# Middle layer normalisation: the fourth deferred projection in a bank of its own, and the small statistics steps on VectorE with only the power left on GpSimd

## The chip, the cores and the metric

One Trainium2 chip, of which the kernel uses one core. The metric is the device time of one launch in microseconds (us), taken as the median of several runs. An execution taken by the profiler has a time of its own; the sums of the prediction are made on that execution.

## The reference, cut to what matters

Two transformer blocks run one after the other on 256 tokens of width 1024, in float32. The first has a mixer, a SwiGLU, another mixer, another SwiGLU and a closing norm; the change does not touch it. The second block is this loop over two layers:

```python
def layer_norm(x, g, b):
    mu = jnp.mean(xf, axis=-1, keepdims=True)
    var = jnp.mean(jnp.square(xf - mu), axis=-1, keepdims=True)
    y = (xf - mu) * lax.rsqrt(var + LN_EPS) * g + b
...
for l in range(DEPTH):
    mix = diff_attention(...) if l == 0 else chunk_attention(...)
    x = layer_norm(DEEPNORM_ALPHA * x + mix, ln_g[l, 0], ln_b[l, 0])
    x = layer_norm(DEEPNORM_ALPHA * x + swiglu_2(x, ffn_w_in[l], ffn_w_out[l]), ln_g[l, 1], ln_b[l, 1])
```

So there are four layer norms. Below they are called norm 0 (behind the first attention), norm 1 (behind the first SwiGLU of this block, the middle one), norm 2 (behind the second attention) and the last norm (behind the last SwiGLU, at the end of the kernel).

## The kernel before, in words

Activations lie with features on the partitions: eight blocks of 128 features by 256 tokens, kept in pairs. Every matmul of a projection is made in three parts to keep float32 precision: the weight is split into `hi` and `lo`, the activation likewise, and `mm3` (lines 245 to 250) issues hi by hi, hi by low activation, and lo by hi. A projection of one 128-feature output block is therefore 8 x 3 = 24 matmuls. `weights` (line 235) loads one weight tile, ScalarE writes `hi` (line 240), VectorE writes `lo` (line 243); `hi` and `lo` have six buffers each, so this work runs some tiles ahead of TensorE.

Accumulators lie in the eight banks of PSUM: three with the tag `pa`, and five for the rest: `s0`, `s1`, `po` (one each) and `tr` (two).

The norms 0 to 2 are objects of the class `Norm` (line 505). While the output blocks of the mixer or SwiGLU in front come out, VectorE forms z, ScalarE forms z times the norm's gain, the two are split, and sums of z and of its square are gathered. Two sets of 128x1 matmuls (line 352) add them over the features. Then come the small steps on a 128x2 tile, one column for each half of the tokens: VectorE copies the sums out of PSUM (`st`, line 527), GpSimd squares the mean, subtracts, floors and adds the epsilon (line 365), raises to the power -1/2 (line 368) and multiplies the mean by the result (`mr`, line 533). TensorE spreads both columns over all partitions with four transposes (`spread`, line 613, into `po`), and ScalarE copies them to `rm` (line 537).

The projections behind a norm do not wait for `rm`. `project` (line 553) runs its 24 matmuls on z times gain, which is not normalised yet, and corrects the result afterwards: VectorE copies two correction columns (`dc`, line 561), multiplies by the reciprocal deviation out of `rm` (line 563, the last reader of the bank), and adds the mean's part (line 564). So a projection's bank stays taken until `rm` is there. `self.tags` is a list of banks for the first projections of a norm, taken one by one in line 554; when it is empty, a projection takes a `pa` bank. Norms 0 and 2 get the list `FOUR`, whose fourth entry is `tr`. Norm 1 gets no list:

```python
    FOUR = ("pa", "pa", "pa", "tr")
    ln = Norm(src, gen, 0, "po", FOUR)
    ln = Norm(ln, ffn(ln, I["v1_0"], I["v3_0"], I["v2_0"], None), 1, 'po')
```

Behind norm 1 stands `chunk_mixer`. Its steps are written out in order: "h0 h1 n0 v0 c0 h2 c1 v1 h3 c2 c3". The step h0 runs four projections (two of keys, two of queries; here p1 to p4), then the scores of four heads; h1 runs four more (p5 to p8); n0 writes the normalised activations themselves (line 548 and 549, on VectorE, held back behind the last query tile of h0); v0 is a projection of the values with them (lines 302 to 304), which takes two `pa` banks at once.

`last_norm` (line 568) ends the kernel; its rows are not deferred. It shares `rpow` (line 362) with the class `Norm`, and these two are all that call it with `floor` set.

The order of the instructions on each engine is made at build time by a list scheduler that plays the program through with its own estimates of durations. Each engine then runs its own list in that order. The program names the engine of each step, the banks, and a few orders such as the one that holds n0 back; the scheduler places the rest.

Of the kernel before, what the change touches and what calls it, by code (L numbers as in the profile page):

```python
# [12 lines left out]
ALU = mybir.AluOpType  # L13
# [150 lines left out]
def model(tc, I, out):  # L164
    with ExitStack() as es:
        _model(es, tc, I, out)


def _model(es, tc, I, out):
    nc = tc.nc  # L170
    V, A, T, G = nc.vector, nc.scalar, nc.tensor, nc.gpsimd
# [10 lines left out]
    class State:  # L182
        def __init__(self):
            self.t = [None] * 4
# [50 lines left out]
    def weights(ap, n):  # L235
        raw = wr.tile([128, n], F32, tag="w", name="raw")
        nc.sync.dma_start(out=raw, in_=ap)
        hi = wh.tile([128, n], F32R, tag="w", name="hi")
        with hold_act():
            A.activation(hi, raw, AF.Copy)  # L240
        lo = wl.tile([128, n], F32R, tag="w", name="lo")
        with hold_dve():
            V.tensor_tensor(out=lo, in0=raw, in1=hi.bitcast(F32), op=ALU.subtract)  # L243
        return hi, lo

    def mm3(ps, hi, lo, k, h, first, last):
        a, b = hi[:, k * 128:k * 128 + 128], lo[:, k * 128:k * 128 + 128]
        T.matmul(ps, a, h[0], start=first, stop=False, skip_group_check=True)  # L248
        T.matmul(ps, a, h[1], start=False, stop=False, skip_group_check=True)  # L249
        T.matmul(ps, b, h[0], start=False, stop=last, skip_group_check=True)  # L250
# [4 lines left out]
    def bank():  # L255
        return pa.tile([128, 2, S], F32, tag="pa", name="pa")

    def att(tag, shape=(128, 512)):
        if tag == "sc":
            turn[0] ^= 1  # L260
            tag = f"s{turn[0]}"
        return pt.tile(list(shape), F32, tag=tag, name=tag, bufs=PB[tag])

    def big(name="b", dt=F32):
        return bp.tile([128, 2, S], dt, tag="big", name=name)
# [41 lines left out]
    def hpair():  # L307
        return [hp.tile([128, 2, S + 2], F32R, tag=t, name=t) for t in ("hh", "hl")]
# [48 lines left out]
    def square(src, n):  # L357
        sq = sp.tile([128, 2, S], F32, tag="sq", name="sq", bufs=4)[:, 0:n]
        A.activation(sq, src, AF.Square)
        return sq  # L360

    def rpow(v, n, eps, floor=False):
        r = sp.tile([128, n], F32, tag="rp", name="rp", bufs=6)
        if floor:
            G.tensor_scalar(out=r, in0=v, scalar1=0.0, scalar2=eps, op0=ALU.max, op1=ALU.add)
        else:
            G.tensor_scalar(out=r, in0=v, scalar1=eps, scalar2=None, op0=ALU.add)
        G.tensor_tensor(out=r, in0=r, in1=mhalf[:, :n], op=ALU.pow)
        return r
# [32 lines left out]
    def two(ap, n=2):  # L402
        return ap.unsqueeze(1).to_broadcast([128, n, S])
# [3 lines left out]
    def ffn(H, w1, w3, w2, rb):  # L407
        gs, acc = [], []

        def down(f0, f1, last):  # L410
            for o, (d0, n) in enumerate(OUT):
                if len(acc) <= o:
                    acc.append(att(("sc", "sc", "tr", "tr", "po")[o], (128, n, S)))
                for j in range(n):
                    hi, lo = weights(w2[d0 + j][:, f0 * 128:f1 * 128], (f1 - f0) * 128)
                    for k in range(f0, f1):
                        mm3(acc[o][:, j], hi, lo, k - f0, gs[k], k + j == 0, last and k == f1 - 1)
                if last:
                    yield d0, n, acc[o]

        def gate(p1, p3, n, bias=None, up=None):
            s = wk.tile([128, 2, S], F32, tag="ev", name="fs", bufs=4)[:, 0:n]
            if bias is not None:
                A.activation(s, p1, AF.Silu, bias=bias)
            elif rb is None:
                A.activation(s, p1, AF.Silu)
            else:
                a = wk.tile([128, 2, S], F32, tag="ev", name="fa", bufs=4)
                V.tensor_tensor(out=a, in0=p1, in1=two(rb), op=ALU.mult)
                A.activation(s, a, AF.Silu)  # L430
                V.tensor_tensor(out=s, in0=s, in1=two(rb), op=ALU.mult)
            gg = wk.tile([128, 2, S], F32, tag="ev", name="fg", bufs=4)[:, 0:n]
            if up is None:
                V.tensor_tensor(out=gg, in0=p3, in1=s, op=ALU.mult)
            else:
                V.scalar_tensor_tensor(out=gg, in0=p3, scalar=up, in1=s, op0=ALU.add, op1=ALU.mult)
            return gg

        def up(f0, f1, H):
            for f in range(f0, f1, 2):  # L440
                p1, p3 = bank(), bank()
                for j in range(2):
                    for ps, w in ((p1, w1), (p3, w3)):
                        hi, lo = weights(w[f + j], 1024)
                        for k in range(8):
                            mm3(ps[:, j], hi, lo, k, H[k], k == 0, k == 7)
                gg = gate(p1, p3, 2)
                g = [big("gh", F32R), big("gl", F32R)]
                split(gg, g)
                gs.extend((g[0][:, j], g[1][:, j]) for j in range(2))  # L450

        def deferred(f0, f1):
            for f in range(f0, f1):
                a, ab = H.project(w1, f)
                b, bb = H.project(w3, f)
                gg = gate(a.unsqueeze(1), b.unsqueeze(1), 1, ab, bb)
                if f % 2 == 0:
                    g = [big("gh", F32R), big("gl", F32R)]
                o = [x[:, f % 2] for x in g]
                split(gg[:, 0], o)  # L460
                gs.append(o)

        for f0, f1 in ((0, 8), (8, 16), (16, NFF)):
            if rb is None:
                deferred(f0, f1)
            else:
                up(f0, f1, H)
            yield from down(f0, f1, f1 == NFF)
            if f0 == 0 and rb is None:
                H.normalize(False)  # L470
# [31 lines left out]
    class Norm:  # L502
        def __init__(self, src, gen, idx, tag, tags=()):
            self.gcol, self.bcol = V_LNG + idx * 8, V_LNB + idx * 8
            self.zg, self.HD = State(), []
            self.tags = list(tags)
            stats = Stats((ncol, mcol), tag)
            for d, n, ps in gen:
                z = wk.tile([128, 2, S], F32, tag="t2", name="z", bufs=3)[:, 0:n]
                V.scalar_tensor_tensor(out=z, in0=src.Y.at(d, n), scalar=ALPHA, in1=ps, op0=ALU.mult, op1=ALU.add)  # L510
                zg = self.zg.at(d, n)
                for j in range(n):
                    A.activation(zg[:, j], z[:, j], AF.Copy, scale=vec[:, self.gcol + d + j:self.gcol + d + j + 1])
                if d % 2 == 0:
                    hl = hpair()
                    for i in range(2):
                        G.tensor_copy(hl[i][:, :, S:S + 2], gbs[i].bitcast(F32)[:, idx, d:d + 2])
                o = [x[:, d % 2:d % 2 + n, 0:S] for x in hl]
                split(zg, o)
                self.HD += [(hl[0][:, (d + j) % 2], hl[1][:, (d + j) % 2]) for j in range(n)]  # L520
                stats.add(0, z, d, n)
                stats.add(1, square(z, n), d, n)
            stats.total(0)
            stats.total(1)
            hold_act.set(recent[1], 3, 3)
            st = sp.tile([128, 4], F32, tag="st4", name="st4")
            V.tensor_copy(st, stats.ps)
            v = sp.tile([128, 2], F32, tag="v2", name="v2", bufs=6)
            G.tensor_tensor(out=v, in0=st[:, 0:2], in1=st[:, 0:2], op=ALU.mult)
            G.tensor_tensor(out=v, in0=st[:, 2:4], in1=v, op=ALU.subtract)  # L530
            r = rpow(v, 2, 1e-5, True)
            mr = sp.tile([128, 2], F32, tag="mr", name="mr")
            G.tensor_tensor(out=mr, in0=st[:, 0:2], in1=r, op=ALU.mult)
            pb = att("po", (128, 2, S))
            spread([r, mr], pb)
            self.rm = wk.tile([128, 2, S], F32, tag="t2", name="rm", bufs=3)
            A.activation(self.rm, pb, AF.Copy)
# [650 lines left out]
    FOUR = ("pa", "pa", "pa", "tr")  # L1188
# [4 lines left out]
    src = Source()  # L1193
    src.Y, gen = diff_mixer(X)
    ln = Norm(src, gen, 0, "po", FOUR)
    ln = Norm(ln, ffn(ln, I["v1_0"], I["v3_0"], I["v2_0"], None), 1, 'po')

    def chunk_mixer(ln):
        v, M, hl = [], [], []
# [85 lines left out]
    ln = Norm(ln, chunk_mixer(ln), 2, "po", FOUR)  # L1285
# [17 lines left out]
```

## Time and profile before

| | us |
|---|---|
| median of 3 runs | 1304.98 (1304.94 to 1304.99) |
| the profiled execution, its own time | 1302.92 |
| its span, first to last instruction | 1301.1 |
| TensorE busy in the span | 1284.6 |
| VectorE busy | 941.3 |
| ScalarE busy | 708.5 |
| GpSimd busy | 45.7 |

Names in the profile: PE is TensorE's matmuls and PEld its weight loads, DVE is VectorE, ACT is ScalarE, POOL is GpSimd, SP is the queue that issues the loads. The profiled execution's own time is 1.82 us above its span, and 2.06 us below the median of the runs. A row of a timeline reads: start in us, duration in us, engine, line, operation, what is written and from what, its shape; xN joins N instructions that follow one another; in square brackets stands how long the engine was idle before it and what ended that. Matmuls overlap one another, so their starts tell more than their durations.

### The profile page before, as it was taken

How to read it: one execution, taken by the hardware profiler on the slowest of the kernel's cores; microseconds unless marked ns; L12 is line 12 of the kernel's file. 1: busy time of each engine (PE TensorE's matmuls, PEld its weight loads, DVE VectorE, ACT ScalarE, POOL GpSimd, SP SyncE). 2: the span in 40 equal slices, each digit the busy share in tenths (PEclk: the TensorE clock that was granted, in tenths of full speed). 3: DMA queues.
4: the chain of work that ended last, by engine and by line, in shares of the span. 5: the costliest groups of instructions: out<-in, count | busy, mean ns of one | idle time of the engine just before them, and what ended most of it. 6: DMA issues, size and time to landing. Idle time of an engine off the chain costs nothing.

```text
span 1301.1 us, 27363 instructions
## 1 busy us (share of the span) xinstructions
PE 1284.6 (99%) x11068; PEld 1240.3 (95%) x11068; DVE 941.3 (72%) x1759; ACT 708.5 (54%) x1185; POOL 45.7 (4%) x99
## 2 busy tenths in 40 slices
PE   9999999999999999999999999999999999999997
PEld 8979999999989999999999899999998889999997
DVE  7896775645888667465678869777779757968676
ACT  6684644434644455343468866544456656554443
POOL 1000000000000000000000021000000000000001
PEclk9999999999999999999999999999999999999999
DMA  9523665655643446565555345565554543655550
GB/s 315 190 82 111 204 201 182 186 183 150 213 155 122 126 167 206 183 186 188 162 178 183 118 130 178 155 209 162 189 174 167 171 138 122 219 187 185 181 158 37
DMA packets 65502, 219.69 MB, mean 169 GB/s; under 512 B 7520, under 2 KB 7904, under 8 KB 65376
## 3 DMA queue, kind: packets, MB, share of 16 engines
q1 hardware_dynamic: 65088, 217.82, 52.4%
q8 instruction: 87, 1.43, 0.4%
q14 instruction: 39, 0.32, 0.1%
q10 hardware_dynamic: 288, 0.12, 0.0%
HBM read 216.86 MB, written 1.05 MB: 167 GB/s over the span
## 4 chain that ended last, share of the span: by engine, by line
PE 97%; ACT 1%; DVE 1%; DMA 0%; issue 0%; SPq 0%; POOL 0%; ACTq 0%; DVEq 0%
PE pa L248 13%; PE pa L249 13%; PE pa L250 13%; PE pd L248 7%; PE pd L250 7%; PE pd L249 7%; PE s L248 4%; PE s L250 4%; PE s L249 4%; PE tr L248 3%; PE tr L249 3%; PE tr L250 3%; PE pv L302 2%; PE pv L303 2%; PE pv L304 2%; PE tr L613 1%
## 5 line engine op out<-in xcount | busy, mean ns | idle before, releaser
L240 ACT ACTIVATE hi<-raw 128x1024 fp32r<-128x1024 f32 (+3 forms) x420 | 424.1, 1018 | 484.8 <-PE pa L249 165.5
L243 DVE TENSOR_TENSOR lo<-raw,hi 128x1024 fp32r<-128x1024 f32 (+3 forms) x420 | 489.9, 1173 | 242.5 <-ACT hi L240 236.4
L248 PE MATMUL pa<-hh,hi 128*128 128x256 f32 x1424 | 401.7, 284 | 0.8 <-DVE ksw L800 0.5
L249 PE MATMUL pa<-hl,hi 128*128 128x256 f32 x1424 | 402.3, 283 | 0.0
L250 PE MATMUL pa<-hh,lo 128*128 128x256 f32 x1424 | 401.2, 283 | 0.0
L249 PEld LDWEIGHTS pa<-hl,hi 128*128 128x128 f32 x1424 | 268.6, 189 | 2.5 <-issue 0.6
L248 PEld LDWEIGHTS pa<-hh,hi 128*128 128x128 f32 x1424 | 267.2, 188 | 3.3 <-issue 1.1
L250 PEld LDWEIGHTS pa<-hh,lo 128*128 128x128 f32 x1424 | 268.6, 189 | 1.4 <-issue 0.7
L250 PE MATMUL pd<-hh,lo 128*128 128x258 f32 x752 | 212.9, 284 | 0.0
L248 PE MATMUL pd<-hh,hi 128*128 128x258 f32 x752 | 211.2, 284 | 1.6 <-DVE y L563 1.6
L249 PE MATMUL pd<-hl,hi 128*128 128x258 f32 x752 | 212.2, 283 | 0.0
L248 PEld LDWEIGHTS pd<-hh,hi 128*128 128x128 f32 x752 | 141.4, 189 | 2.0 <-DVE y L563 1.9
L249 PEld LDWEIGHTS pd<-hl,hi 128*128 128x128 f32 x752 | 142.8, 190 | 0.0
L250 PEld LDWEIGHTS pd<-hh,lo 128*128 128x128 f32 x752 | 142.2, 189 | 0.2
L250 PE MATMUL s<-gh,lo 128*128 128x256 f32 x352 | 97.4, 279 | 0.0
L249 PE MATMUL s<-gl,hi 128*128 128x256 f32 x352 | 97.4, 279 | 0.0
L248 PE MATMUL s<-gh,hi 128*128 128x256 f32 x352 | 95.8, 279 | 0.0
L249 PE MATMUL tr<-gl,hi 128*128 128x256 f32 x264 | 73.8, 280 | 0.0
L248 PE MATMUL tr<-gh,hi 128*128 128x256 f32 x264 | 73.8, 279 | 0.0
L250 PE MATMUL tr<-gh,lo 128*128 128x256 f32 x264 | 73.7, 279 | 0.0
L250 PEld LDWEIGHTS s<-gh,lo 128*128 128x128 f32 x352 | 65.9, 188 | 0.0
L249 PEld LDWEIGHTS s<-gl,hi 128*128 128x128 f32 x352 | 65.9, 187 | 0.0
(360 smaller groups left out, 1903.5 us busy)
## 6 DMA issues: line engine op xcount, KB each, us to landing
raw<-w SPq DMA_DIRECT2D x120, 512.0 KB, 3.8
raw<-v SPq DMA_DIRECT2D x120, 512.0 KB, 4.0
raw<-w_e SPq DMA_DIRECT2D x18, 512.0 KB, 4.8
raw<-w_aqk SPq DMA_DIRECT2D x16, 512.0 KB, 3.6
raw<-w SPq DMA_DIRECT2D x16, 384.0 KB, 3.2
raw<-v SPq DMA_DIRECT2D x16, 384.0 KB, 3.2
raw<-w_of SPq DMA_DIRECT2D x8, 512.0 KB, 4.2
raw<-w_oq SPq DMA_DIRECT2D x8, 512.0 KB, 3.6
```

The source lines that it names most:

```text
L240: A.activation(hi, raw, AF.Copy)
L243: V.tensor_tensor(out=lo, in0=raw, in1=hi.bitcast(F32), op=ALU.subtract)
L248: T.matmul(ps, a, h[0], start=first, stop=False, skip_group_check=True)
L249: T.matmul(ps, a, h[1], start=False, stop=False, skip_group_check=True)
L250: T.matmul(ps, b, h[0], start=False, stop=last, skip_group_check=True)
L302: T.matmul(ps[t], xh, a, start=k == 0, stop=False)
L303: T.matmul(ps[t], xh, b, start=False, stop=False)
L304: T.matmul(ps[t], xl, a, start=False, stop=k == 7)
L613: T.transpose(ps, src, ident)
```

## The change

In `rpow`, the step that floors the variance and adds the epsilon moves from GpSimd to VectorE where `floor` is set. In `Norm`, the square of the mean, the subtraction and the product `mr` move from GpSimd to VectorE; the power stays on GpSimd. Norm 1 gets the list `FOUR`, so its fourth projection takes a `tr` bank in place of a `pa` bank.

```diff
     def rpow(v, n, eps, floor=False):
         r = sp.tile([128, n], F32, tag="rp", name="rp", bufs=6)
         if floor:
-            G.tensor_scalar(out=r, in0=v, scalar1=0.0, scalar2=eps, op0=ALU.max, op1=ALU.add)
+            V.tensor_scalar(out=r, in0=v, scalar1=0.0, scalar2=eps, op0=ALU.max, op1=ALU.add)
...
-            G.tensor_tensor(out=v, in0=st[:, 0:2], in1=st[:, 0:2], op=ALU.mult)
-            G.tensor_tensor(out=v, in0=st[:, 2:4], in1=v, op=ALU.subtract)
+            V.tensor_tensor(out=v, in0=st[:, 0:2], in1=st[:, 0:2], op=ALU.mult)
+            V.tensor_tensor(out=v, in0=st[:, 2:4], in1=v, op=ALU.subtract)
             r = rpow(v, 2, 1e-5, True)
             mr = sp.tile([128, 2], F32, tag="mr", name="mr")
-            G.tensor_tensor(out=mr, in0=st[:, 0:2], in1=r, op=ALU.mult)
+            V.tensor_tensor(out=mr, in0=st[:, 0:2], in1=r, op=ALU.mult)
...
-    ln = Norm(ln, ffn(ln, I["v1_0"], I["v3_0"], I["v2_0"], None), 1, 'po')
+    ln = Norm(ln, ffn(ln, I["v1_0"], I["v3_0"], I["v2_0"], None), 1, "po", FOUR)
```

## Rows read from the trace of the kernel before

**Rows 1.** The page: busy time by engine, and the chain by engine.

```profile
PE 1284.6 (99%) x11068; PEld 1240.3 (95%) x11068; DVE 941.3 (72%) x1759; ACT 708.5 (54%) x1185; POOL 45.7 (4%) x99
...
PE 97%; ACT 1%; DVE 1%; DMA 0%; issue 0%; SPq 0%; POOL 0%; ACTq 0%; DVEq 0%
```

**Rows 2.** Stretches: length, then busy us of PE, PEld, DVE, ACT, POOL.

```profile
780.00:950.00 170.00, 170.00 (x1422) 170.00 (x1421) 133.81 (x246) 88.89 (x125) 3.97 (x7) 1.00 0.57 177
...
985.00:992.00 7.00, 5.17 (x40) 4.55 (x39) 5.89 (x14) 6.22 (x11) 1.20 (x2) 1.00 0.85 287
...
1000.00:1010.00 10.00, 10.00 (x60) 8.65 (x59) 10.00 (x31) 6.20 (x13) 0.00 (x0) 1.00 0.45 150
...
1100.00:1280.00 180.00, 180.00 (x1511) 180.00 (x1510) 138.27 (x255) 90.22 (x123) 3.02 (x5) 1.00 0.54 170
```

**Rows 3.** Who waited for whom, TensorE: total us, times, longest.

```profile
PE pd L248 <- DVE y L563: 1.6, 1, 1.6
```

**Rows 4.** Timeline of TensorE at norm 1.

```profile
985.50 0.28 PE L250 MATMUL pd<-hh,lo 128*128 128x258 f32 x1
...
986.33 0.43 PE L613 MATMUL po<-ident,mr 128*128 128x128 f32 x2 [0.19 <-POOL mr L533]
988.40 0.39 PE L248 MATMUL pd<-hh,hi 128*128 128x258 f32 x1 [1.64 <-DVE y L563]
...
991.40 0.28 PE L248 MATMUL pd<-hh,hi 128*128 128x258 f32 x1
```

**Rows 5.** Timeline of TensorE at norm 0.

```profile
792.78 0.28 PE L248 MATMUL tr<-hh,hi 128*128 128x258 f32 x1
...
794.07 0.38 PE L613 MATMUL po<-ident,mr 128*128 128x128 f32 x2
...
796.09 0.29 PE L248 MATMUL pd<-hh,hi 128*128 128x258 f32 x1
```

**Rows 6.** Timeline of GpSimd at norms 0 and 1.

```profile
789.23 1.10 POOL L529 TENSOR_TENSOR v<-st 128x2 f32<-128x2 f32 x1 [6.76 <-DVE st L527]
...
791.82 0.77 POOL L533 TENSOR_TENSOR mr<-st,rp 128x2 f32<-128x2 f32 x1
...
984.07 0.20 POOL L529 TENSOR_TENSOR v<-st 128x2 f32<-128x2 f32 x1 [27.15 <-DVE st L527]
...
984.93 0.72 POOL L368 TENSOR_TENSOR rp<-rp,mhalf 128x2 f32<-128x2 f32 x1
985.73 0.54 POOL L533 TENSOR_TENSOR mr<-st,rp 128x2 f32<-128x2 f32 x1
```

**Rows 7.** Timeline of VectorE at norms 0 and 1, and behind norm 1.

```profile
789.07 1.22 DVE L243 TENSOR_TENSOR lo<-raw,hi 128x1024 fp32r<-128x1024 f32 x1
...
795.12 1.09 DVE L563 TENSOR_TENSOR y<-pd,rm 128x256 f32<-128x256 f32 x3
...
983.83 0.15 DVE L527 COPY st<-po 128x4 f32<-128x4 f32 x1
...
987.93 1.08 DVE L563 TENSOR_TENSOR y<-pd,rm 128x256 f32<-128x256 f32 x3
...
991.60 0.16 DVE L561 COPY dc<-pd 128x2 f32<-128x2 f32 x1 [0.62 <-PE pd L250]
...
1005.97 0.42 DVE L563 TENSOR_TENSOR y<-pd,rm 128x256 f32<-128x256 f32 x1
```

**Rows 8.** Timeline of ScalarE at norm 1: the copy that makes `rm`.

```profile
986.80 0.60 ACT L537 ACTIVATE rm<-po 128x512 f32<-128x512 f32 x1
```

**Rows 9.** Timeline of TensorE: the value projection's second bank.

```profile
1006.78 0.40 PE L302 MATMUL pv<-hi,hh 128*128 128x512 f32 x1
```

**Rows 10.** Timeline of all engines in the last norm.

```profile
1291.57 0.16 DVE L586 TENSOR_TENSOR v<-s,v 128x2 f32<-128x2 f32 x1
...
1292.24 1.88 DVE L597 TENSOR_TENSOR x<-x,pa 128x512 f32<-128x512 f32 x3 [0.52 <-ACT sb L590]
...
1292.88 0.43 PE L613 MATMUL pa<-ident,rp 128*128 128x128 f32 x2 [1.09 <-POOL rp L368]
```

## The prediction

> **What bounds the kernel now.** The page comes first. TensorE is busy for 1284.6 us of the 1301.1 us span, and the chain that ended last is TensorE for 97% [rows 1]. So a change on another engine is worth only the time for which TensorE stands still because of it, and the question is where TensorE stands still near a layer norm. The stretches answer that: from 780 to 950 us, which holds norm 0, and from 1100 to 1280 us, which holds norm 2, TensorE is busy all the time; from 985 to 992 us, at norm 1, it is busy for 5.17 of 7.00 us [rows 2]. The list of waits names the cause: one wait of 1.6 us of a projection's first matmul for VectorE's line 563 [rows 3]. The timeline shows it in place. The last matmul of the third projection (p3) starts at 985.50, the transposes of `mr` start at 986.33 after 0.19 us of waiting, and the fourth projection (p4) starts at 988.40, when line 563 has read the first of three `pa` banks [rows 4]. The first of the three joined reads that free the banks starts at 987.93, behind the ScalarE copy of `rm`, which ends at 987.40 [rows 7, 8]. At norm 0 the fourth projection writes `tr` and no such gap is there [rows 5]; norm 2 repeats that pattern once more.
>
> **The change part by part.**
>
> *The bank.* It removes p4's wait for a `pa` bank; no load is moved or added, and no queue of loads is touched. What is left is TensorE's own pace. At norm 0, p4 with the four transposes inside it takes from 792.78 to the start of the fifth projection at 796.09, that is 3.31 us [rows 5]. At norm 1, p4 could start one pitch behind 985.50; p4's own 24 matmuls, from 988.40 to p5's start at 991.40 [rows 4], follow one another at 3.00 / 24 = 0.12 us. Then p5 starts at 985.50 + 0.12 + 3.31 = 988.93 in place of 991.40 [rows 4]: **2.47 us earlier**. The idle time summed over the stretch is smaller, 7.00 - 5.17 = 1.83 us [rows 2], because a matmul's recorded end reaches past the start of its successor. The starts decide, since p5 cannot begin sooner than they allow. The Trainium skill says as much in "Trainium Kernel Development and Optimization", section Performance Expectations: matmul busy time is a poor measure because matmuls are pipelined; by busy time the sum would be 1.83, by starts it is 2.47, and the 0.64 us between them are in these rows.
>
> Who is late next at p5? It takes the first `pa` bank, free once the first of the three joined reads has ended: 987.93 + 1.08 / 3 = 988.29 at today's pace [rows 7]. That is 0.64 us before 988.93, so p5 doesn't wait even if `rm` comes no earlier than now.
>
> *The small steps.* Today GpSimd needs from the end of `st` at 983.98 to the end of `mr` at 985.73 + 0.54 = 986.27, that is 2.29 us at norm 1 [rows 6, 7]. At norm 0 its chain runs from 789.23 to 792.59, 3.36 us, since its first step alone takes 1.10 in place of 0.20 us [rows 6]. On VectorE a step of this size takes 0.16 us [rows 10]; four of them are 0.64, with the power's 0.72 and some 0.3 for gaps and two hand-overs (an estimate from the 0.09 us between `st` and GpSimd's first step and the 0.08 between the power and `mr`) the chain would be about 1.7 us, 0.6 shorter. Nobody on TensorE needs that time: at norms 0 and 2 it never stands still, and at norm 1 the fourth bank covers it. I cost this part at **nothing** in itself. If the cover were gone, its 0.6 us would be a gain at norm 1 only. VectorE gets 3 x 4 + 1 = 13 steps more, 2.1 us in all, on an engine that is busy 72% [rows 1]. The new wait is `mr`, which now stands in VectorE's queue behind the power: behind it are `lo` tiles, which TensorE needs several tiles later, and the reads of the `pa` banks, which need `mr` anyway.
>
> *The last norm.* Its floor step moves to VectorE, which sits idle for 0.52 us just there, and costs 0.16. The power's result is spread over the partitions by 1293.31, but VectorE is busy with three additions until 1294.12 before it can use it [rows 10]. So this is worth **0**; bounds are 0.1 us of gain, about the hand-over saved, and 0.6 of loss, one addition (1.88 / 3) put ahead of the step.
>
> *What p5 to p8 meet.* From here TensorE runs 2.47 us earlier, and VectorE is the next to be late: between 1000 and 1010 us it is busy for 10.00 of 10.00 us [rows 2]. The tightest place is the value projection, which takes two `pa` banks. Its second starts to be written at 1006.78, and line 563 ends reading that bank at 1005.97 + 0.42 = 1006.39 [rows 7, 9]: 0.39 us to spare. VectorE's own work can move up by the 0.62 us that it waits for p4 [rows 7] and by the 0.53 between `rm` and the first read at 987.93, less up to 0.64 for new steps: 0.5 to 1.15 us. If both engines kept their order, TensorE would be short by 2.47 - 0.39 - 1.15 = 0.9 to 2.47 - 0.39 - 0.5 = 1.6 us there. But the scheduler, which plays out the whole order anew, has work to fill this with: the first bank's further blocks (each three matmuls) and a read that can be put ahead of VectorE's other work. The bounds are 0 and 1.6; I take **0.4 us given back**, nearer to 0 because the shortage is one bank for a short time and not a shortage of VectorE's total.
>
> Sum: -2.47 + 0 + 0 + 0.4 = -2.07 us. The profiled execution would go from 1302.92 to 1300.85; the runs lie 2.06 us above it, so the median goes from 1304.98 to **1302.9**.
>
> About 0.2% (2.6 us) is what a measurement of this kernel can tell from no change; the forecast is a gain of 0.16%.
>
> **The rivals.**
>
> *Nothing given back.* The scheduler fills the value projection's gap and the tail gives its 0.1 us: 2.47 + 0.1 = 2.57, so 1302.4. For it: in the later stretches read, TensorE is busy throughout, so nothing else stops it [rows 2]. Against it: VectorE has no free time at all from 1000 to 1010 us [rows 2].
>
> *VectorE gives most of it back.* Both engines keep their order behind p5 and the whole 1.6 us is lost: 2.47 - 1.6 = 0.9 us gained, 1304.1. For it: only 0.39 us of room at the second value bank [rows 7, 9]. Against it: the room to reorder.
>
> *Slower: the moved steps queue behind `lo` tiles.* VectorE's list has a `lo` of 1.22 us every tile. In the trace, the GpSimd step that starts at 789.23, while VectorE makes a `lo` from 789.07 to 790.29, ends at 790.33, and the same step without one beside it takes 0.20 [rows 6, 7]. So the power may still be held for 1.22 us by a `lo` put directly behind the floor step, and each moved step may stand behind another. The Trainium skill's "GPSIMD Engine Reference", section Key points, says that GpSimd shares its SBUF interfaces with VectorE and contends with instructions that have two SBUF inputs; these two rows agree. With four `lo` in between the chain is 4 x 1.22 + 0.64 + 0.72 = 6.2 us. At norm 1 `mr` then comes at 983.98 + 6.2 = 990.2; spreading (0.43), copying (0.60) and one read (0.36) [rows 4, 7, 8] free the bank at 991.6, and p5 waits 2.7 us: 0.2 us worse than today. At norms 0 and 2 the transposes of `mr` now come 794.07 - 792.59 = 1.48 us after it is ready, and the first read ends at 795.48, 0.61 before p5 [rows 5 to 7]; a chain 2.8 us longer than the 3.36 uses this up and costs 0.7 at each. With the 0.4 from above: +0.2 + 1.4 + 0.4 = 2.0 us slower, 1307.0. It decides from a chain of some 3.5 us at norm 1 and 5.5 at the others. Against it: VectorE has 1.1 us free in the stretch from 985 to 992 us [rows 2], so not every bubble between two small steps needs to be filled by a `lo`.
>
> *The change doesn't do what it says* in one respect: `rm` may come no earlier, as the power is held once. The chain is then about 2.9 us, below 3.5, and the forecast stands.
>
> **How the numbers follow.** Chances: the forecast (gains of 1.2 to 2.6 us) 0.60, nothing given back 0.18, most of it given back 0.14, slower 0.08. The range leaves out the far ends: it reaches from 1302.2, a little beyond the full gain, to 1305.2, past the second rival into the first of the slower outcomes. Faster by over 0.2% takes half of the second case and some of the first: 0.13. Slower by over 0.2% takes less than half of the last: 0.03. The rest, 0.84, is within 0.2%.
>
> **What would show it.** In the changed kernel p4 writes `tr`, the wait of rows 3 is gone, and p5 starts some 3.4 us behind the end of p3. At norm 1 the steps from `st` to `mr` take 1.7 to 2.9 us with 0.16 for each VectorE step. Around the value projection a new wait of TensorE for line 563 of up to 1.6 us would be the part given back. TensorE busy throughout at norms 0 and 2 would show the small steps to be free. The prediction is wrong if p5 waits at norm 1, if TensorE stands still at norms 0 or 2, or if idle time of TensorE comes up further on, behind the value projection, where I expect the order to be as good as now.

## The result, and the profile after

The changed kernel takes 1311.65 us in the median of 4 runs (1310.74 to 1312.43), the kernel before 1304.96 us (1303.43 to 1304.99, 4 runs). The ratio is 1.0058, with an interval of 1.0046 to 1.0070: **slower by 0.58%**, where a gain of 0.16% was forecast. The profiled execution took 1311.43 us with a span of 1309.6 us, 8.5 us more than the span of before.

The page of the changed kernel, busy time and chain, answers to [rows 1]:

```profile
PE 1288.6 (98%) x11068; PEld 1244.9 (95%) x11068; DVE 942.9 (72%) x1772; ACT 708.6 (54%) x1185; POOL 41.4 (3%) x86
...
PE 95%; ACT 2%; DVE 1%; issue 1%; DMA 0%; POOL 0%; SPq 0%; ACTq 0%; DVEq 0%
```

The 13 steps stand where they were put: VectorE has 1772 instructions in place of 1759, GpSimd 86 in place of 99. TensorE's share of the chain fell from 97% to 95%. The list of waits of the changed kernel, in answer to [rows 3], says at once where:

```profile
PE pd L248 <- DVE y L563: 7.0, 3, 2.4
```

One wait of 1.6 us has become three of 7.0 us together, one at each norm. The stretches that answer to [rows 2] (length, busy us of PE, PEld, DVE, ACT, POOL, then the granted clock), and three short ones right behind the three waits:

```profile
780.00:950.00 170.00, 167.73 (x1388) 167.51 (x1387) 131.15 (x242) 86.94 (x122) 2.64 (x3) 0.99 0.55 173
...
799.00:802.40 3.40, 3.40 (x19) 3.40 (x18) 3.40 (x7) 0.00 (x0) 0.00 (x0) 0.52 0.51 171
...
995.50:999.00 3.50, 3.50 (x30) 3.50 (x30) 3.43 (x11) 3.34 (x7) 0.00 (x0) 1.00 0.82 277
...
1100.00:1280.00 180.00, 177.72 (x1477) 177.51 (x1476) 139.67 (x261) 92.26 (x131) 1.73 (x1) 0.99 0.54 170
...
1120.00:1123.50 3.50, 3.50 (x19) 3.50 (x18) 3.26 (x7) 0.00 (x0) 0.00 (x0) 0.51 0.40 150
```

At norms 0 and 2, where TensorE was busy throughout, it now stands still for 2.27 and 2.28 us. Behind both waits the granted clock is 0.52 and 0.51, the 1.2 GHz level, and there are 19 matmuls in some 3.4 us; behind the wait at norm 1 it stays at 1.00, the 2.4 GHz level, with 30 matmuls in 3.5 us.

TensorE's timeline of the changed kernel at norm 0 and, in the last two rows, at norm 1 [rows 4, 5]:

```profile
792.65 0.28 PE L248 MATMUL tr<-hh,hi 128*128 128x258 f32 x1
...
795.42 0.28 PE L250 MATMUL tr<-hh,lo 128*128 128x258 f32 x1
795.55 0.38 PE L613 MATMUL po<-ident,rp 128*128 128x128 f32 x2
795.76 0.38 PE L613 MATMUL po<-ident,mr 128*128 128x128 f32 x2
...
798.42 0.36 PE L248 MATMUL pd<-hh,hi 128*128 128x258 f32 x1 [2.27 <-DVE y L563]
...
799.26 0.42 PE L248 MATMUL pd<-hh,hi 128*128 128x258 f32 x1
799.48 0.42 PE L249 MATMUL pd<-hl,hi 128*128 128x258 f32 x1
...
992.61 0.38 PE L613 MATMUL po<-ident,mr 128*128 128x128 f32 x2
...
995.39 0.39 PE L248 MATMUL pd<-hh,hi 128*128 128x258 f32 x1 [2.40 <-DVE y L563]
```

The thing to see is where the four transposes (L613) stand. Before, at norm 0, they lay inside p4. Now p4 runs from 792.65 to 795.42 without a break, and the transposes come behind its last matmul. Then TensorE has nothing to do until `rm` has been copied and a bank read, at 798.42.

VectorE at norm 0 of the changed kernel [rows 7]:

```profile
788.87 0.15 DVE L527 COPY st<-po 128x4 f32<-128x4 f32 x1
788.94 1.22 DVE L243 TENSOR_TENSOR lo<-raw,hi 128x1024 fp32r<-128x1024 f32 x1
790.08 0.15 DVE L529 TENSOR_TENSOR v<-st 128x2 f32<-128x2 f32 x1
...
791.18 1.22 DVE L243 TENSOR_TENSOR lo<-raw,hi 128x1024 fp32r<-128x1024 f32 x1 [0.74 <-ACT hi L240]
792.33 0.16 DVE L365 TENSOR_SCALAR rp<-v 128x2 f32<-128x2 f32 x1
792.49 1.23 DVE L243 TENSOR_TENSOR lo<-raw,hi 128x1024 fp32r<-128x1024 f32 x1
...
794.31 0.16 DVE L533 TENSOR_TENSOR mr<-st,rp 128x2 f32<-128x2 f32 x1 [0.52 <-POOL rp L368]
...
796.71 1.22 DVE L243 TENSOR_TENSOR lo<-raw,hi 128x1024 fp32r<-128x1024 f32 x1 [0.81 <-ACT hi L240]
797.85 1.08 DVE L563 TENSOR_TENSOR y<-pd,rm 128x256 f32<-128x256 f32 x3
```

GpSimd's power at norm 0, and the same at norm 1 [rows 6]:

```profile
792.57 1.71 POOL L368 TENSOR_TENSOR rp<-rp,mhalf 128x2 f32<-128x2 f32 x1 [10.22 <-DVE dc L561]
...
988.63 0.69 POOL L368 TENSOR_TENSOR rp<-rp,mhalf 128x2 f32<-128x2 f32 x1 [27.82 <-DVE rp L365]
```

VectorE at norm 1, the `lo` that starts while that power runs:

```profile
988.89 1.23 DVE L243 TENSOR_TENSOR lo<-raw,hi 128x1024 fp32r<-128x1024 f32 x1 [0.34 <-ACT hi L240]
```

ScalarE at norm 0, ahead of and at the copy of `rm` [rows 8]:

```profile
795.62 1.06 ACT L240 ACTIVATE hi<-raw 128x1024 fp32r<-128x1024 f32 x1 [1.83 <-DVE lo L243]
796.59 0.58 ACT L537 ACTIVATE rm<-po 128x512 f32<-128x512 f32 x1
```

So the hand-over from `st` to p5 at norm 0 has six links, and most of them meet a tile of the weights: a `lo` ahead of the first small step (1.14 us from 788.94 to 790.08); 0.74 us of waiting for a `hi`, and its `lo`, ahead of the floor step (at 792.33); a `lo` that starts just ahead of the power (1.71 us, where the power takes 0.69 at norm 1); p4's matmuls ahead of the transposes (`mr` has been ready since 794.47, the transposes of `mr` come at 795.76, 1.29 us later); a `hi` ahead of the copy (until 796.59); 0.81 us of waiting and one more `lo` ahead of the first read (from 797.17, when `rm` is there, to 797.85).

All kernels below are laid out by the same measure: the start of `st` at a norm is set to zero, and the starts of the later links are counted from there (us, from the timelines; "ahead" is how many of p4's 24 matmuls stand in TensorE's list ahead of the transposes of `mr`):

```
                 norm 0: mr done  transposes  p5     ahead | norm 1: mr done  transposes  p5     ahead
before                   3.60     5.08        7.10   9     |         2.44     2.50        7.57   0
changed                  5.60     6.89        9.55   24    |         2.53     4.89        7.67   24
bank_only                as before                         |         2.45     4.77        7.46   23
steps_only               as changed                        |         2.53     2.58        7.56   0
mr_back                  6.24     6.89        9.55   24    |         2.44     4.65        6.18   22
mr_only                  3.61     6.04        7.66   17    |         2.53     4.88        7.45   24
lo_behind                2.55     4.95        7.72   8     |         1.73     4.21        6.74   12
after_tr                 5.60     5.80        7.42   15    |         2.53     3.08        5.12   9
bank_tr                  as before                         |         2.45     3.09        5.12   9
```

p5 at norm 2 repeats norm 0 within 0.02 us in these kernels. And the span (to the end of the last instruction, in hundredths), cut at the three `st`, each piece less that of before (before: 788.99, 194.84, 121.25 and 196.05 us):

```
              to norm 0   norm 0 to 1   norm 1 to 2   norm 2 to end   sum
changed        -0.12        +4.01         +0.63          +3.99        +8.5
bank_only      +0.08        -0.01         +1.40           0.00        +1.5
steps_only     +0.23        +2.52          0.00          +2.48        +5.2
mr_back        +0.62        +3.94         -0.09          +3.98        +8.4
mr_only        -0.08        +0.79         +0.34          +0.84        +1.9
lo_behind      +0.79        +0.48         +1.77          +1.25        +4.3
after_tr       +0.09        +0.41         -4.03          +0.36        -3.2
bank_tr        +0.02        -0.01         -4.07          +0.01        -4.1
after_tr02     +0.69        +0.41         +1.60          +0.37        +3.1
```

Up to norm 0 TensorE's order is that of before in all of these but lo_behind, so the first column, up to 0.69 us, shows how far two executions differ by themselves.

The loss is now in two nearly equal halves, norm 0 and norm 2. At norm 0, 4.01 us is 9.55 - 7.10 = 2.45 us of later p5, and 1.43 us of matmuls at the lower clock: 15 of them, from 799.26 on, follow one another at 0.215 us in place of 0.12, and 15 x 0.095 = 1.43. Norm 1, where the gain was to be, gives +0.10 at p5.

### The profile page after: what moved, and what is told of

Read it like the earlier page. It is cut to its first block, busy times and chain, and to the rows that moved or that the text cites. A ratio compares the mean times of both kernels' runs of the same rounds, so it can differ in the third digit from the quotient of the medians.

```text
span 1309.6 us, 27361 instructions
## 1 busy us (share of the span) xinstructions
PE 1288.6 (98%) x11068; PEld 1244.9 (95%) x11068; DVE 942.9 (72%) x1772; ACT 708.6 (54%) x1185; POOL 41.4 (3%) x86
## 3 DMA queue, kind: packets, MB, share of 16 engines
q8 instruction: 87, 1.43, 0.4%
## 4 chain that ended last, share of the span: by engine, by line
PE 95%; ACT 2%; DVE 1%; issue 1%; DMA 0%; POOL 0%; SPq 0%; ACTq 0%; DVEq 0%
PE pa L248 13%; PE pa L249 13%; PE pa L250 13%; PE pd L248 7%; PE pd L249 7%; PE pd L250 7%; PE s L248 4%; PE s L250 4%; PE s L249 4%; PE tr L248 2%; PE tr L249 2%; PE tr L250 2%; PE pv L302 2%; PE pv L303 2%; PE pv L304 2%; PE tr L613 1%
```

## The experiments

**Each half alone.** The first two kernels make one half of the change each: bank_only has the last line of the diff, steps_only the four others.

```diff
-    ln = Norm(ln, ffn(ln, I["v1_0"], I["v3_0"], I["v2_0"], None), 1, 'po')
+    ln = Norm(ln, ffn(ln, I["v1_0"], I["v3_0"], I["v2_0"], None), 1, "po", FOUR)
```

> Only the bank: the small steps stay on GpSimd, norm 1 gets the list FOUR. Theory Q (the list scheduler's places decide): at norm 1 the four transposes now stand behind 23 of p4's 24 matmuls in TensorE's list, so the bank moves the wait from p4 to p5; p5 starts where it did, within 0.7 us, and the time is 1304.3 to 1305.5. Rival B (the bank is good by itself and all of the loss is the moved steps'): p5 starts about 2.5 us sooner and the time is 1302.5 to 1303.3.

> Only the moved steps: norm 1 keeps three banks. Theory Q: norms 0 and 2 lose as in the changed kernel, some 2.4 us of waiting and 1.4 us of slow clock each, norm 1 is within 0.5 us of the kernel before; 1312 to 1313.5. Rival B' (the bank at norm 1 shifts what follows and makes part of the loss at norm 2): below 1309.

Measured, against 1304.38 us of the kernel before (1302.64 to 1305.74, 21 runs): bank_only 1303.43 us (1302.52 to 1305.08), ratio 0.9996 [0.9987, 1.0005], no change; steps_only 1310.81 us (1308.15 to 1310.96), ratio 1.0047 [1.0034, 1.0061]. So the small steps carry the loss, and the bank brings nothing. Both came out below the times expected of theory Q (1304.3 to 1305.5 and 1312 to 1313.5); the places of the transposes and the start of p5 came out as it said. TensorE's timeline of bank_only at norm 1:

```profile
988.67 0.38 PE L613 MATMUL po<-ident,mr 128*128 128x128 f32 x2
...
991.36 0.39 PE L248 MATMUL pd<-hh,hi 128*128 128x258 f32 x1 [2.19 <-DVE y L563]
```

and the stretch of bank_only behind it (columns as above):

```profile
993.00:995.50 2.50, 2.50 (x14) 2.50 (x13) 1.27 (x5) 1.27 (x3) 0.00 (x0) 0.50 0.84 290
```

p4 does start at once, but the transposes now stand behind 23 of its matmuls, 2.27 us later than before (4.77 against 2.50), with `mr` as early as ever. p5 starts at 991.36, before at 991.40: the wait moved from p4 to p5 and kept its end. The +1.40 us that the profiled run of bank_only has from norm 1 to norm 2 is the fall of the clock behind that wait (0.50, 14 matmuls in 2.5 us). steps_only's profiled run has the pieces free of any fall of the clock: +2.52 and +2.48 at norms 0 and 2, nothing at norm 1. TensorE in steps_only at norm 0:

```profile
798.78 0.36 PE L248 MATMUL pd<-hh,hi 128*128 128x258 f32 x1 [2.27 <-DVE y L563]
```

and the stretch behind that:

```profile
799.00:802.40 3.40, 3.40 (x30) 3.40 (x30) 3.40 (x7) 0.58 (x1) 0.00 (x0) 1.00 0.66 224
```

The same wait, and the clock stays at 2.4 GHz. This profiled run took 1308.15 us, the other three runs 1310.80 to 1310.96, some 2.7 us more: about two falls of 1.43. That those runs had them is a reading of the sum only, since they have no trace.

**Which small step.** mr_back is the changed kernel with `mr` back on GpSimd; mr_only is bank_only with `mr` alone on VectorE.

```diff
-            V.tensor_tensor(out=mr, in0=st[:, 0:2], in1=r, op=ALU.mult)
+            G.tensor_tensor(out=mr, in0=st[:, 0:2], in1=r, op=ALU.mult)
```

> The changed kernel with the product mr back on GpSimd, so VectorE has no step that waits for the power. Theory Q: the three steps ahead of the power still stand between lo tiles, and the transposes still stand at the end of p4; 1310.5 to 1312.5, with waits of about 2.3 us at norms 0 and 2. Rival W (the wait of mr for the power in VectorE's list is what costs): the waits at norms 0 and 2 go, 1304 to 1306.

> Only mr on VectorE, the three steps ahead of the power on GpSimd, with the fourth bank. Theory Q: the chain up to the power is that of before (2.75 us at norms 0 and 2); the transposes of mr stand behind 17 of p4's matmuls there in place of 9, some 1 us later, with at most 1 us of waiting at p5 for each: 1304 to 1307. Rival W (VectorE standing still behind the power is the cost): waits of 2 us at norms 0 and 2, 1309 or more.

mr_back: 1312.65 us (1311.36 to 1312.73), ratio 1.0064 [1.0050, 1.0078], no better than the change as it was and 0.15 us above the range expected; its waits at norms 0 and 2 are 2.27 and 2.28 us. mr_only, beside another set of runs of the kernel before (1303.24 us, 1302.55 to 1304.99, 16 runs): 1305.07 us (1304.65 to 1306.84), ratio 1.0013 [1.0004, 1.0022], inside its range. The waits in mr_back:

```profile
PE pd L248 <- DVE y L563: 5.5, 3, 2.3
...
PE pv L304 <- DVE hl L314: 1.3, 1, 1.3
```

In mr_back `mr` is ready 0.64 us later than in the changed kernel (6.24 against 5.60), and the transposes start at the same 6.89: the time of `mr` doesn't matter while 24 matmuls stand in front. (At norm 1 p5 starts 1.39 us sooner in mr_back than in before, and the value projection then waits 0.74 and 1.33 us; the second wait is the last line above.) In mr_only the chain to `mr` is that of before to 0.01 us (3.61), yet p5 at norm 0 is 0.56 later, because the transposes moved from behind 9 matmuls to behind 17. Two kernels, then, in which chain and loss don't go together, and the place of the transposes and the loss do.

**A shorter chain.** lo_behind is the changed kernel with three `lo` tiles, those of p6 to p8, held in VectorE's list until `mr` is issued, so that none stands between the small steps.

```diff
-            V.tensor_tensor(out=mr, in0=st[:, 0:2], in1=r, op=ALU.mult)
+            hold_dve.set(V.tensor_tensor(out=mr, in0=st[:, 0:2], in1=r, op=ALU.mult), 5, 3)
```

> The changed kernel, with the next three lo tiles held behind mr in VectorE's list, so that no lo stands between the small steps or runs beside the power. Theory Q: the chain from st to mr shrinks to 1.6 to 2 us, the transposes stand behind 8 (norms 0 and 2) and 12 (norm 1) matmuls of p4, no wait is left at norms 0 and 2, p5 at norm 1 starts 1.5 to 2.5 us sooner than before: 1302.5 to 1303.6. Rival P (the hand-overs to and from GpSimd cost what the moved steps save): waits of over 1 us stay at norms 0 and 2, above 1307.

1306.59 us (1304.67 to 1308.12), ratio 1.0020 [1.0011, 1.0029]: two thirds of the loss are gone, but it is no gain. Neither side had it right: theory Q said 1302.5 to 1303.6, rival P waits of over 1 us at norms 0 and 2. VectorE in lo_behind at norm 0:

```profile
792.17 0.16 DVE L533 TENSOR_TENSOR mr<-st,rp 128x2 f32<-128x2 f32 x1 [0.81 <-POOL rp L368]
...
795.80 1.22 DVE L243 TENSOR_TENSOR lo<-raw,hi 128x1024 fp32r<-128x1024 f32 x1
796.93 1.08 DVE L563 TENSOR_TENSOR y<-pd,rm 128x256 f32<-128x256 f32 x3
```

and TensorE at norm 0 and at the value projection behind norm 1:

```profile
797.50 0.36 PE L248 MATMUL pd<-hh,hi 128*128 128x258 f32 x1 [0.44 <-DVE y L563]
...
1007.12 0.47 PE L302 MATMUL pv<-hi,hh 128*128 128x512 f32 x1 [0.90 <-DVE ng L1220]
...
1009.30 0.73 PE L304 MATMUL pv<-hi,hl 128*128 128x512 f32 x2 [1.48 <-DVE hl L314]
```

From the end of `st` the chain to `mr` takes 2.40 us at norm 0 and 1.58 at norm 1, where the prediction had 1.7, and the list has the transposes behind 8 and 12 matmuls. But a `lo` now stands ahead of the first read (795.80), so p5 is still 0.62 us late at norm 0 and 0.58 at norm 2. At norm 1 p5 gains 0.83 us counted from `st`; since `st` itself comes 0.76 us sooner in TensorE's order here (the last matmul of p3 starts 2.43 us behind it, in before 1.67), p5 gains 1.59 us on TensorE, and the table's +0.48 for norm 0 to 1 is too small by the same 0.76. All of it is lost again at the value projection, where VectorE comes 0.90 and 1.48 us late, and behind these waits to the clock, which was granted at 0.50 from 1010.25 to 1013.50. This kernel shortened the chain and moved the transposes together, so it doesn't tell the two apart. The next two do.

**The place of the transposes alone.** after_tr is the changed kernel, bank_tr is bank_only, with one order written out: p4's later matmuls may only be issued behind the transposes. In after_tr these then stand behind 15, 9 and 15 of p4's matmuls at norms 0, 1 and 2; in bank_tr behind 9 at norm 1 and as before at the others. The engines of the steps and the banks are untouched; the scheduler again places the rest around that order.

```diff
-            spread([r, mr], pb)
+            self.spread, self.first = spread([r, mr], pb), (3 if idx == 1 else 5)
...
-                mm3(ps, hi, lo, k, self.HD[k], k == 0, k == 7)
+                with tc.issue_after(self.spread.ins) if tag == "tr" and k >= self.first else nullcontext():
+                    mm3(ps, hi, lo, k, self.HD[k], k == 0, k == 7)
```

> The changed kernel, with p4's matmuls from the 16th on (norms 0 and 2) or the 10th on (norm 1) held behind the four transposes in TensorE's list; VectorE and GpSimd keep the moved steps. Theory Q (the place of the transposes in the list is the larger part of the loss, the longer chain the smaller): from the end of mr at 5.6 us behind st the transposes follow at once, the read of the first bank ends near 7.1, and p5 waits 0.5 us or less at norms 0 and 2, with no slow clock; p5 at norm 1 is 2 to 2.5 us sooner than before, and the value projection behind it gives 1 to 2.5 us back: 1303 to 1305.5. Rival C (the chain itself, lengthened by lo tiles and the held power, is the loss): waits of over 1.5 us stay at norms 0 and 2, above 1308.

> Only the bank, steps on GpSimd, and at norm 1 p4's matmuls from the 10th on held behind the transposes (norms 0 and 2 keep their order). Theory Q: p5 starts 2 to 2.5 us sooner; from there VectorE decides, the value projection waits for its normalised inputs or banks by 1 us or more, and the whole gains 0.3 to 1.5 us: 1302.9 to 1304.1 where the kernel before gives 1304.4. Rival F (what the prediction took: 0.4 us given back): a gain of about 2 us, 1302.4 or less on the same chip.

after_tr: **1299.83 us** (1299.77 to 1300.1), ratio 0.9970 [0.9959, 0.9982]. bank_tr: **1299.02 us** (1298.85 to 1299.54), ratio 0.9965 [0.9951, 0.9978], the fastest kernel of this study. For after_tr, rival C is out: no wait of over 0.2 us is left at norms 0 and 2. Both are faster than theory Q had it (1303 to 1305.5, and 1302.9 to 1304.1), which took 1 us or more to be given back at the value projection; for bank_tr the time falls on rival F's side, 1302.4 or less. Beside each other, after_tr is 0.81 us slower than bank_tr, with no overlap of their runs: even with the transposes in a good place, the moved steps cost more than they save. TensorE in after_tr at norms 0 and 1:

```profile
794.88 0.38 PE L615 MATMUL po<-ident,mr 128*128 128x128 f32 x2
...
796.50 0.36 PE L248 MATMUL pd<-hh,hi 128*128 128x258 f32 x1 [0.16 <-DVE y L565]
...
987.41 0.38 PE L615 MATMUL po<-ident,mr 128*128 128x128 f32 x2
...
989.45 0.28 PE L248 MATMUL pd<-hh,hi 128*128 128x258 f32 x1
```

Its chain to `mr` is that of the changed kernel to the hundredth, 5.60 and 2.53 us. With the transposes 1.09 us earlier at norm 0 (5.80 against 6.89), p5 is 2.13 us earlier (7.42 against 9.55), since the copy and the first read now also come ahead of the `hi` and `lo` that they stood behind. The place of before, behind 9 matmuls, could not have been kept without a wait, as `mr` comes 2.00 us later; behind 15 is soon enough. So of the 2.45 us at norm 0, 2.13 are the transposes' place with what follows from it, and 0.32 the longer chain itself. At norm 1 p5 is 2.55 us earlier than in the changed kernel (5.12 against 7.67). The gain of the bank is there with the moved steps too; the list gave it away. TensorE in bank_tr, at norm 1 and at the scores of the second pair of heads:

```profile
988.96 0.28 PE L248 MATMUL pd<-hh,hi 128*128 128x258 f32 x1
...
1001.64 0.71 PE L1216 MATMUL s<-bk,bq 64*128 64x256 f32 x4
1002.18 0.39 PE L1217 MATMUL s<-bk,bq 64*128 64x128 f32 x4
1002.50 0.50 PE L302 MATMUL pv<-hi,hh 128*128 128x512 f32 x1
...
1003.86 0.50 PE L304 MATMUL pv<-hi,hl 128*128 128x512 f32 x1 [0.62 <-DVE hl L314]
```

p5 at 988.96 is the prediction's 988.93 to 0.03 us. The stretch from norm 1 to norm 2 gains more than that, though: 4.07 us.

**How far each norm counts.** after_tr02 is after_tr with the order at norms 0 and 2 only.

```diff
-            self.spread, self.first = spread([r, mr], pb), (3 if idx == 1 else 5)
+            self.spread, self.first = spread([r, mr], pb), (8 if idx == 1 else 5)
```

> The changed kernel with the transposes pulled forward at norms 0 and 2 alone (norm 1 keeps the scheduler's place, behind 22 and 24 of p4's matmuls). Theory Q (each norm pays for its own list): norms 0 and 2 lose 0.5 us or less in place of 3.9, norm 1 is as in the changed kernel and within 0.5 us of the kernel before: 1303.8 to 1305.5. Rival N (the pull at norm 1 also carries part of what norms 0 and 2 got back): 1307 or more.

1305.29 us (1303.89 to 1306.01), ratio 1.0004 [0.9995, 1.0014] against 1304.32 us (1303.12 to 1305.24, 21 runs): no change, inside theory Q's range. The pieces agree with after_tr's at norms 0 and 2 (+0.41 and +0.37), and at norm 1 p5 starts 7.67 us behind `st` again, as in the changed kernel. Its waits, and the stretch behind the wait of 2.40 us at norm 1:

```profile
PE pd L248 <- DVE y L565: 2.6, 2, 2.4
...
993.75:997.25 3.50, 3.50 (x19) 3.50 (x18) 1.76 (x6) 1.98 (x5) 0.23 (x2) 0.51 0.72 270
```

Here the clock fell behind that wait (0.51), where in the changed kernel it stayed at 1.00 behind a wait of the same 2.40 us; most of the +1.60 us from norm 1 to norm 2 is this fall.

**The rest of bank_tr's gain.** 4.07 - (7.57 - 5.12) = 1.62 us are gained between p5 and norm 2. The rows of before that differ are score matmuls, which use one half of TensorE's rows each:

```profile
1000.36 0.70 PE L1214 MATMUL s<-bk,bq 64*128 64x256 f32 x2
1000.89 0.38 PE L1215 MATMUL s<-bk,bq 64*128 64x128 f32 x2
1001.21 0.39 PE L250 MATMUL pd<-hh,lo 128*128 128x258 f32 x1
...
1002.12 0.70 PE L1214 MATMUL s<-bk,bq 64*128 64x256 f32 x2
```

The trace has two records for each of these float32 matmuls (32 at line 1214 for 16 heads), so four records are one head and eight are a pair; the two heads of a pair use the two halves of the rows. In before the four records of one head run from 1000.36 to 1001.21, 0.85 us, and those of the other head, torn off, take the same again from 1002.12. In bank_tr the eight stand together and take 0.86 us, from 1001.64 to 1002.50. The Trainium skill's "TensorE: Matmul & The Clock Gate", Part 3, says that matmuls on different row tiles of the array run at the same time; these rows agree. Of the eight pairs in this layer, before has three torn, the changed kernel four, bank_tr and after_tr one. From start to next start, the score rows take 9.38 us in before, 10.21 in the changed kernel and 7.71 in bank_tr and after_tr. So of the 4.07 us that bank_tr gains from norm 1 to norm 2, 1.67 stand in the score rows, and all other rows and waits of TensorE together give 2.40, about the 2.45 of p5: the sum of rows places the 1.62 us in the pairs. One pair more torn, 0.83, stands against the 0.53 us that the changed kernel loses between p5 and norm 2. Two kernels were to test it, by issuing both heads' score matmuls in turn: before_pair in the kernel before, bank_tr_pair in bank_tr.

```diff
-            pp = att("sc", (128, 384))
-            T.matmul(pp[:, 0:256], q[r, 128:256], k[r], start=True, stop=True)
-            T.matmul(pp[:, 256:384], q[r, 0:128], k[r, 0:128], start=True, stop=True)
...
+                for j in (1, 0):
+                    with tc.issue_after(ins.ins) if ins else nullcontext():
+                        ins = T.matmul(pps[j][:, 0:256], q[rows[j], i, 128:256], k[rows[j], i], start=True, stop=True)
```

> The kernel before, with the score matmuls of two heads issued in turn (upper 64 rows, lower 64 rows) in place of one head after the other. Theory S (two heads' 64-row score matmuls run side by side when they are neighbours in TensorE's list; three pairs of the eight are torn apart in the list of before and cost 0.86 us more each): 1.7 to 3 us faster, about 1301. Rival O (the 1.6 us that the pulled kernels gain behind p5 come from elsewhere, such as fewer changes between float32 and split matmuls): within 0.6 us of before.

> The bank with the transposes pulled forward at norm 1, steps on GpSimd, and the two heads' score matmuls in turn. Theory S: one torn pair of the eight is mended, 0.5 to 1.2 us less than without, about 5 us below the kernel before on the same chip. Rival O: within 0.4 us of the version without.

1309.07 us (1307.24 to 1309.95), ratio 1.0034 [1.0021, 1.0046], and 1305.93 us (1304.35 to 1308.53), ratio 1.0016 [1.0007, 1.0024]. Neither gained, against both theories: S had said 1.7 to 3 us faster and about 5, O within 0.6 and 0.4 us. In either one of the eight pairs is still torn, and the score rows do shrink as theory S says, to 7.45 us. But the new order also re-placed the work around norm 2: p5 there starts 9.22 us behind `st` in place of 7.12 in before_pair, and 10.66 in bank_tr_pair. The waits in before_pair have a line that only these two kernels have:

```profile
PE pd L248 <- issue: 1.2, 1, 1.2
```

After that wait (at 1099.23 and 1096.15) the clock fell in both: it was granted at 0.50 from 1106.3 to 1109.6 in before_pair, and from 1098.25 to 1111.75 in bank_tr_pair, with TensorE busy throughout. So the test is not clean: that whole pairs save time on TensorE rests on the sum of rows, and no run here changed the pairs alone.

## Why the prediction was wrong

**The step that failed is "The small steps", and in it the sentence "Nobody on TensorE needs that time: at norms 0 and 2 it never stands still".** It took TensorE's list at norms 0 and 2, with the transposes inside p4, for a thing that stays. The list is made anew at every build. With the small steps in VectorE's list, the transposes went from behind 9 of p4's matmuls to behind 24, and TensorE stood still for 2.27 us with nothing left to do; the prediction's own signs of being wrong, TensorE standing still at norms 0 or 2 and p5 waiting at norm 1, both came. steps_only shows the loss (+2.52 and +2.48 us, and the change's 6.7 us nearly whole in the median). after_tr and after_tr02 show the cause: same steps, same chain, transposes earlier, and the loss at norms 0 and 2 falls from 4.01 and 3.99 us to 0.41 and 0.37. Even so the steps are not worth the nothing that they were put at: those two pieces, 0.8 us together, remain. Why the scheduler's estimates put the transposes there was not looked into.

**"The chain would be about 1.7 us, 0.6 shorter"** failed too: 2.38 us at norm 1 from the end of `st`, against 2.29 before, and 5.45 at norm 0 against 3.45. At norm 0 two `lo` stand between the small steps and one beside the power, where the sum had 0.3 us for gaps; at norm 1 a `lo` that starts at 988.89 keeps `mr` until 990.10, though the power ends at 989.32. But this is the smaller error, 0.32 us of p5 at norm 0 once the transposes are in place.

**The bank, -2.47 us:** the mechanism and the size were right where the list lets it work: in bank_tr p5 starts 2.44 us sooner. Without that it is worth next to nothing: p5 starts 0.11 us sooner in bank_only, and 0.10 us later in the changed kernel, counted from `st`. The step "p5 doesn't wait even if `rm` comes no earlier" rested on the same unspoken assumption: it took norm 0's p4, transposes inside, for norm 1, and `rm` then came 3.0 us later (transposes at 4.89 and copy at 5.93 us from `st`, before 2.50 and 2.97).

**The last norm, 0:** right. From norm 2 to the end the changed kernel loses 3.99 us, of which p5 has 2.43 and the clock 1.43.

**p5 to p8, 0.4 us given back:** right in kind, and not the whole of it. Where p5 came sooner, a wait of 0.62 us showed up at the value projection (bank_tr), where before had none; in mr_back it was 2.1 us and in lo_behind 2.4, beyond the upper bound of 1.6. But in bank_tr the new order also kept two more pairs of heads whole, which the prediction had no term for, so nothing was given back in the end: it gains 4.2 us in the median (1303.24 to 1299.02), twice the 2.07 forecast.

**The rivals.** "Slower: the moved steps queue behind `lo` tiles" had the right sign and the right place for the first link, with the power held by a `lo` as it said. Its price was short: it put the loss at 2.0 us in all, and at norm 0 its own point of decision, 5.5 us of chain, would have left the measured 5.45 free. It was short because it let only the chain to `mr` grow and kept the places of the transposes, of the copy and of the first read, and because it had no price for the clock (1.43 us at each of two norms).

## What to carry to other kernels

Where a list scheduler places the work, an edit on one engine re-places its consumers on all others: cost a hand-over link by link to its last reader, and for each link ask what the new list may put in front, rather than keep the places that the old trace shows. A stretch in which the busiest engine never stands still proves only that the old order hid the hand-over. And where a transfer between engines gates the next stage, write its order out by hand: here that turned a ratio of 1.0058 into 0.9970 with the change, and 0.9996 into 0.9965 with the bank alone. The moved steps were not what gained: with both orders written out, the kernel without them was the faster one.

## What the runs showed of the hardware

- GpSimd's power on a 128x2 tile takes 0.69 us at norm 1, where no `lo` has started ahead of it, and 1.71 us when a `lo` has started 0.08 us ahead of it: 792.57 to 794.28, 0.56 us past the end of the `lo` at 793.72. The Trainium skill's "SBUF — State Buffer", section "SBUF: two separate sides", calls the port pair that VectorE and GpSimd share an exclusive lock, held for the whole instruction by whichever came first. The rows agree where the `lo` came first. Where the power came first they do not: the `lo` that starts 0.26 us into it, at 988.89, takes 1.23 us like the others, so here only the small op pays.
- TensorE's granted clock fell from 2.4 to 1.2 GHz behind some waits of 2.2 to 2.4 us and not behind others of the same length: it fell behind 2.27 and 2.28 us in the changed kernel, 2.19 us in bank_only and 2.40 us in after_tr02, and stayed behind 2.40 us in the changed kernel, 2.27 and 2.28 us in steps_only and 2.18 us in mr_only. In lo_behind it fell behind two waits of 0.90 and 1.48 us. The falls at norms 0 and 2 of the changed kernel lasted some 3.2 us each, in which 15 matmuls cost 1.43 us more.
- The score matmuls of two heads (eight records), on the two halves of the rows, take 0.86 us together; those of one head alone (four records) take 0.85 us.
